# A step of the state-space scan: state increments ahead of the 64-column products, sums of squares behind them

## The chip, the core and the metric

The kernel runs on one core of a Trainium2 chip. The metric is the device time of one execution in microseconds. A core has five engines with queues of their own that run at the same time and wait for each other on semaphores: TensorE (PE, matrix products into PSUM), VectorE (DVE), ScalarE (ACT), GpSimd (POOL) and SyncE (SP, which here issues DMA transfers).

## The reference

One layer of a decoder trunk over 1024 tokens of width 1024. The part that the change touches is the chunked state-space scan (SSD), with 8 groups of 4 heads, head width 64, state 128:

```python
cb = jnp.einsum('bclgn,bcsgn->bcgls', cc, bc)
y_diag = jnp.einsum('bcgls,bcgrls,bcsgrp->bclgrp', cb, decay, xd)
decay_to_end = jnp.exp(a_cs[..., -1:] - a_cs)
chunk_states = jnp.einsum('bcsgn,bcgrs,bcsgrp->bcgrpn', bc, decay_to_end, xd)
...
    return state * cd[..., None, None] + cs, state          # scan over chunks
...
y_off = jnp.einsum('bclgn,bcgrpn,bcgrl->bclgrp', cc, prev_states, jnp.exp(a_cs))
y = y_diag + y_off
...
y_b = rms_norm(yz.reshape(..., SSM_GROUPS, -1), ssm_norm_w)  # yz = (y + x*d_skip) * silu(z)
merged = sigmoid(g_a) * (y_a @ w_proj_a) + sigmoid(g_b) * (y_b @ w_proj_b)
return x + gate * (merged @ w_out)
```

Chunks are 128 tokens long; B, C, x and z come from the input projection, which runs before.

## The kernel before

The program has a long first part (norm, input projection, convolution, gates; up to about 915 us), then the SSD stage (about 915 to 1145 us), then the projection of y_b and the output product. The change reorders instructions in the SSD stage and renames PSUM banks in it and behind it.

**Steps.** The stage has 32 steps, one for each of 8 groups and 4 spans of 256 tokens (two chunks). Groups go in pairs: `order` lists (g, s) with the two groups of a pair in turn. In step n the loop calls, for its own and for later steps, the pieces of class `Group`:

- `decay_rows` of step n+3: ACT's exponentials `ea`, and POOL's mask (an affine_select) on the tile `dcy` of decays;
- `front` of step n: PE forms `yi`, the products inside the chunks (8 of 64 columns, xd against dcy), and `sp`, the increments of the state (2 of 256 columns, bn against xe); DVE writes `y` from yi and x (two instructions) and adds the first half of sp to the state `st`; POOL multiplies the state by the next chunk's decay (`decayed`);
- a few pieces of the first projection, y_a @ w_proj_a (`draw`: pairs of products `pma` of 512 columns, 4 or 5 a step), which need nothing of the scan;
- `prep_xe` of step n+1: DVE makes `xe` (x times the decay to the end of the chunk) from the transposed x in PSUM (`px`), and frees px's bank;
- `back` of step n: PE forms `yn` from the states, DVE multiplies it by ea (`ym`), POOL adds it to y; DVE adds the second half of sp, POOL decays the state and makes `yz`; every second time `post` plans what follows from yz;
- `prep_products` of step n+2: PE forms C times B and transposes B (both into `pc`) and x (into `px`); DVE multiplies dcy by pc and makes `xd`;
- `decay_exps` of step n+3 and `prep_b` of step n+2: ACT's exponentials on dcy, and its copy `bn` of the transposed B;
- `fetch` of step n+6: SP loads dcy and the operands `sl`.

**Order.** PE and SP run in the order in which the code emits, and in this stage so do DVE, ACT and POOL (`Engine` keeps the program's order). The order of the code is thus the order on each engine; what waits, holds up all that is behind it on its engine. Two high-and-low pairs of the projection's weights are split beside the steps: `wah` by ACT, `wal` by DVE (two instructions, in six of the steps), and SP loads them.

**Tasks.** `later(delay, f)` plans f for `delay` items ahead; a step has three items (front, back, prep_products). `post` plans the squares of yz (ACT, and their sum on POOL), `post2` (PE: `pq`, the sums over channels, 4 products of 32 columns), then `post2b` (DVE: a row of sums into cwt, tri or par), the row's store to `ss_d` and load as `ssq` (SP), POOL's power, and the store to `rs_d`. The groups 6 and 7 have shorter delays (`soon = 4`).

**Banks.** PSUM has eight banks, held in the list `free`, which begins as BANKS. `bank(name)` takes the first of the list, `release` puts a bank at its end. A product into a bank therefore waits for whoever used the bank last, and a change of the order of `bank` and `release` changes who that is. Behind the stage, `places_of` says which bank each product of the second projection takes.

The line L91 of the profile is the helper `mm` (a product), L94 is `tp` (a transpose), L100 is `move` (a DMA on SP), and L56 is the wrapper through which DVE, ACT and POOL instructions are recorded, so there tiles tell them apart, not lines. A product of 32-bit operands shows as two rows on PE.

Of the kernel before, what the change touches and what calls it, by code (L numbers as in the profile page):

```python
# [8 lines left out]
F32 = mybir.dt.float32  # L9
# [3 lines left out]
ALU = mybir.AluOpType  # L13
# [3 lines left out]
P = 128  # L17
# [3 lines left out]
NCH = S // P  # L21
# [14 lines left out]
def hybrid_kernel(  # L36
# [21 lines left out]
    V, A, G, PE = Engine(nc.vector), Engine(nc.scalar), Engine(nc.gpsimd), nc.tensor  # L58
    ctx.enter_context(nc.allow_non_contiguous_dma(reason="small parameter vectors"))

    x, out = x[0], out[0]
# [23 lines left out]
    def cst(shape, name, dt=F32):  # L85
        return const.tile(shape, dt, name=name, tag=name)
# [3 lines left out]
    def mm(acc, l, r, first=True, last=True):  # L90
        pin(PE.matmul(acc, l, r, start=first, stop=last))  # L91

    def tp(dst, src, idn):
        pin(PE.transpose(dst, src, idn))  # L94
# [4 lines left out]
    def move(dst, src):  # L99
        pin(nc.sync.dma_start(dst, src))  # L100
# [6 lines left out]
    ident = cst([P, P], "ident")  # L107
# [21 lines left out]
    dskt = cst([P, 16], "dskt")  # L129
# [13 lines left out]

    hpool = tc.tile_pool(name="hpool", bufs=1, reuse_waits="tile")
    hp = hpool.__enter__()
    BANKS = (1, 4, 6, 0, 3, 5, 2, 7)
    BN = ("b11", "t1", "t2", "b22", "t3", "b21", "t4")
    bop = {}
    for nm in BN:
# [338 lines left out]
    def bank(name):  # L488

        if not free and not at_bank:  # L490
            return psum.tile([P, 512], F32, name=name, tag="bk", bufs=6)
        at_bank[name] = free.pop(0)
        return psum.tile([P, 512], F32, name=name, tag=f"k{at_bank[name]}")

    def release(*names):

        free.extend(at_bank.pop(name) for name in names if name in at_bank)

    def numbered(pool, c):
        for b in range(8):  # L500
            pool.tile([P, 512], F32, name=f"{c}{b}_0", tag=f"{c}{b}")
# [4 lines left out]
    def later(delay, f, *a):  # L506
        tasks.append((slot[0] + delay, f, a))
# [557 lines left out]
    class Group:  # L1065
# [50 lines left out]
        def prep_products(self, s):  # L1116
            g, nm = self.g, f"{self.g}_{s}"
            sl, dcy, ea = self.pre[s]
            px, pc = bank(f"px{nm}"), bank(f"pc{nm}")
            for i in range(2):  # L1120
                tsl = slice(i * P, (i + 1) * P)
                mm(pc[:, i * P : (i + 1) * P], sl[:, 1, tsl], sl[:, 0, tsl])
                tp(pc[:, 256 + i * P : 256 + (i + 1) * P], sl[:, 1, tsl], ident)
                tp(px[:, i * 256 : i * 256 + P], sl[:, 2, tsl], ident)
                tp(px[:, i * 256 + P : i * 256 + 256], sl[:, 3, tsl], ident)
            d3 = dcy.rearrange("p h i l -> p h (i l)")
            V.tensor_tensor(d3, d3, pc[:, 0:256].unsqueeze(1).to_broadcast([P, HPG, 256]), op=ALU.mult)
            self.raw[s] = px, pc
            self.xs[s] = [self.weighted(s, "xd", dthq)]
# [30 lines left out]
        def front(self, s):  # L1160

            g, nm = self.g, f"{self.g}_{s}"
            sl, dcy, ea = self.pre[s]
            bn, (xd, xe) = self.bn[s], self.xs[s]
            yi = bank(f"yi{nm}")
            for i in range(2):
                for h in range(HPG):
                    j, hh = h // 2, h % 2
                    mm(yi[hh * HD : (hh + 1) * HD, j * 256 + i * P : j * 256 + (i + 1) * P],
                       xd[:, i * 256 + h * HD : i * 256 + (h + 1) * HD], dcy[:, h, i, :])  # L1170
            sp = bank(f"sp{nm}")
            last = s == NCH // 2 - 1
            for i in range(1 if last else 2):
                mm(sp[:, i * 256 : (i + 1) * 256], bn[:, i * P : (i + 1) * P], xe[:, i * 256 : (i + 1) * 256])
            self.y[s] = y1 = turn(y1_r, f"y1{nm}", F32).rearrange("p (j t) -> p j t", j=2)
            for j in range(2):
                V.scalar_tensor_tensor(y1[:, j], sl[:, 2 + j], dskt[:, 2 * g + j : 2 * g + j + 1],
                                       yi[:, j * 256 : (j + 1) * 256], op0=ALU.mult, op1=ALU.add)
            self.sts = [self.st]
            if self.st is None:  # L1180
                self.st = self.state(f"st{nm}_0")
                V.tensor_copy(self.st, sp[:, 0:256])
            else:
                self.st = self.nxt
                V.tensor_add(self.st, self.st, sp[:, 0:256])
            self.sts.append(self.st)
            self.nxt = None
            release(f"yi{nm}")
            if last:
                release(f"sp{nm}")  # L1190
            else:
                self.nxt = self.state(f"st{nm}_1"), sp
                self.decayed(self.nxt[0], s, 1)
# [30 lines left out]
        def post(self, q):  # L1224

            g = self.g
            yz = self.yz[q]

            def leave():
                for j in range(2):  # L1230
                    move(yb_d[2 * g + j][:, q * 512 : (q + 1) * 512], yz[:, j])

            if g < NG - 2 or q == 0:
                soon = 0 if g < NG - 2 else 4
                later(4, leave)
                later(9 - soon, self.squares, yz, [yz[:, j] for j in range(2)])
                later(17 - 2 * soon, self.post2, q, yz[:, 0])
            else:
                wait = 1 if g < NG - 1 else 3
                later(wait + 3, leave)  # L1240
                sq = [turn(r, f"sq{g}", F32) for r in ((y1_r, ym_r) if g < NG - 1 else (war_r[0], war_r[0]))]
                later(wait, self.squares, yz, sq, pin)
                later(9, self.post2, q, sq[0])
# [71 lines left out]
    def take(name, tag=None, dt=F32R):  # L1315
        return hp.tile([P, 512], dt, name=name, tag=tag or room.pop(0))

    def ring(n):

        return [room.pop(0) for _ in range(n)], [0]  # L1320

    def turn(r, name, dt=F32R):
        tags, at = r
        at[0] += 1
        return take(name, tags[(at[0] - 1) % len(tags)], dt)
# [170 lines left out]
    tha_r, ea_r, y1_r, ym_r = (ring(c) for c in (4, 3, 2, 2))  # L1496
# [11 lines left out]
    numbered(psum, "k")  # L1508
    free.extend(BANKS)
    for k in (6, 7):  # L1510
# [249 lines left out]
    ps3 = tc.tile_pool(name="ps3", bufs=1, space=PSUM, reuse_waits="tile")  # L1760
    psb = ps3.__enter__()
    numbered(psb, "q")
    places_of = {"x": (1, 3, 2, 0), "y": range(4, 8)}
    assert all(b > 3 for b in free[6:])
    wo, wor = {}, {}
    KO = (4, 5, 6, 7, 0, 1, 2, 3)
# [90 lines left out]
    def inv_root(sq):  # L1857

        y, t, v = sq[:, 2:3], sq[:, 3:4], sq[:, 1:2]
        V.tensor_scalar(t, sq[:, 0:1], 1.0 / D, EPS, op0=ALU.mult, op1=ALU.add)  # L1860
        V.tensor_scalar(y.bitcast(I32), t.bitcast(I32), -0.5, float(0x5F3759DF), op0=ALU.mult, op1=ALU.add)
        V.tensor_scalar_mul(v, t, -0.5)
        for _ in range(3):
            V.scalar_tensor_tensor(t, y, y, v, op0=ALU.mult, op1=ALU.mult)
            V.scalar_tensor_tensor(y, t, 1.5, y, op0=ALU.add, op1=ALU.mult)
        return y
# [24 lines left out]
    for n, t in enumerate(tiles):  # L1891
        tsl = slice(t * P, (t + 1) * P)
# [5 lines left out]
        last = n == NCH - 1  # L1898
# [15 lines left out]
        if last:  # L1914
            V.scalar_tensor_tensor(sq[:, 0:1], part[:, 0:1], part[:, 1:2], part[:, 2:3], op0=ALU.add, op1=ALU.add)
            y = inv_root(sq)
# [4 lines left out]
        else:  # L1921
            V.tensor_add(r, pw, xr)
            A.activation(xr, r, AF.Square, accum_out=sq[:, 0:1])  # L1923
            y = inv_root(sq)
# [35 lines left out]
```

## Time and profile before

| | |
|---|---|
| median of 3 runs | 1393.12 us (1393.1 to 1395.72) |
| profiled execution | 1396.63 us |
| its span | 1394.9 us, granted clock 0.999 |
| PE busy | 1370.1 us (98%) |
| DVE / ACT / POOL busy | 1032.8 / 771.2 / 211.5 us |
| HBM read and written | 195.63 and 83.30 MB |

Busy time is the time in which an engine runs an instruction; the span is from the first to the last. An engine with a busy share near 100% sets the time; the idle time of the others is spent waiting, mostly for it. The timeline's columns are start, duration, engine, line, operation, output and inputs, size and count, and in brackets the idle time ahead of it, with what ended it.

### The profile page before, as it was taken

What the parts mean: (1) busy time and instruction counts of PE and PEld (TensorE: products, weight loads), DVE (VectorE), ACT (ScalarE), POOL (GpSimd) and SP (SyncE); (2) the same over time, 40 slices, a digit from 0 to 9 for tenths busy, and PEclk for the clock granted to TensorE, in tenths of its full rate; (3) what the DMA queues carried; (4) which work ended last, traced back from release to release, by engine and by line L of the source; (5) the groups of instructions that cost most, each with busy time, mean ns of one, the idle gap of its engine ahead of it and who ended that gap; (6) DMA issues with size and microseconds to landing.
All of it is one profiled execution on the core that took longest, in us unless ns stands there. A gap on an engine that the chain in (4) does not pass through costs nothing.

```text
span 1394.9 us, 20349 instructions
## 1 busy us (share of the span) xinstructions
PE 1370.1 (98%) x7015; PEld 1131.3 (81%) x7015; DVE 1032.8 (74%) x1771; ACT 771.2 (55%) x1420; POOL 211.5 (15%) x198
## 2 busy tenths in 40 slices
PE   8999999999999999999999999999999999999997
PEld 6678888888888888888888788888888878888886
DVE  4666766776677789878988877577888768787743
ACT  6664456566556666555656555577777724233301
POOL 0000000000000000000000010018888860000000
PEclk9999999999999999999999999999999999999999
DMA  8565533333322567677667876598899859987332
GB/s 265 154 223 160 176 110 112 108 99 111 117 91 91 158 183 210 208 245 241 207 207 219 253 226 178 179 333 294 290 316 293 261 148 294 411 263 273 136 121 76
DMA packets 268907, 280.28 MB, mean 201 GB/s; under 512 B 18396, under 2 KB 215428, under 8 KB 268804
## 3 DMA queue, kind: packets, MB, share of 16 engines
q1 hardware_dynamic: 193796, 211.20, 48.3%
q10 hardware_dynamic: 75008, 67.78, 14.3%
q8 instruction: 55, 0.90, 0.3%
q14 instruction: 48, 0.39, 0.1%
HBM read 195.63 MB, written 83.30 MB: 200 GB/s over the span
## 4 chain that ended last, share of the span: by engine, by line
PE 86%; DMA 4%; DVE 3%; ACT 2%; issue 2%; POOL 1%; SPq 1%; POOLq 0%; DVEq 0%; ACTq 0%
PE xx L591 6%; PE xuz L591 6%; PE xcb L591 6%; PE po L91 6%; PE xz L591 6%; PE xg L591 5%; PE x L1680 5%; PE pma L91 4%; PE yp L1680 3%; PE yuz L591 3%; PE ycb L591 3%; PE yx L591 3%; PE vx L703 3%; PE yz L591 3%; PE yg L591 3%; PE vy L703 2%
## 5 line engine op out<-in xcount | busy, mean ns | idle before, releaser
L923 POOL TENSOR_TENSOR wog<-wog,gb 128x1024 f32<-128x1024 f32 x8 | 22.6, 2830 | 647.1 <-DMA wbr<-in_w_proj_b_dram 450.0
L56 ACT ACTIVATE dcy<-dcy,nacs 128x128 f32<-128x128 f32 x256 | 78.3, 388 | 16.9 <-POOL dcy L56 16.4
L56 POOL TENSOR_SCALAR_AFFINE_SELECT dcy<-dcy 128x1024 f32<-128x1024 f32 x32 | 36.4, 1138 | 102.1 <-DVE yh L56 61.3
L91 PE MATMUL pma<-yh,wah 128*128 128x512 f32 x128 | 42.9, 416 | 0.0
L91 PE MATMUL pma<-yh,wal 128*128 128x512 f32 x128 | 42.6, 414 | 0.0
L56 ACT ACTIVATE ea<-dcy 64x512 f32<-64x512 f32 x64 | 40.3, 629 | 4.0 <-DMA dcy<-acs_d 3.5
L56 POOL TENSOR_TENSOR yz<-y,sl 128x512 f32<-128x512 f32 x32 | 41.3, 1290 | 0.6
L56 DVE TENSOR_TENSOR dcy<-dcy,pc 128x1024 f32<-128x1024 f32 x32 | 39.0, 1218 | 2.7 <-PE pc L94 1.8
L1014 ACT ACTIVATE ac<-ac 128x1024 f32<-128x1024 f32 x32 | 34.0, 1061 | 12.6 <-DVE ac L1012 12.4
L56 DVE TENSOR_TENSOR ym<-yn,ea 128x512 f32<-128x512 f32 (+1 forms) x32 | 19.9, 621 | 27.8 <-PE yn L91 27.7
L91 PE MATMUL pma<-yl,wah 128*128 128x512 f32 x128 | 39.9, 393 | 0.0
L56 POOL TENSOR_TENSOR y<-y,ym 128x512 f32<-128x512 f32 (+1 forms) x32 | 36.6, 1143 | 15.3 <-DVE ym L56 15.0
L91 PE MATMUL yi<-dcy,xd 128*64 128x128 f32 x512 | 35.0, 279 | 2.8 <-DVE xe L56 2.5
L1923 ACT ACTIVATE xr<-r 128x1024 f32<-128x1024 f32 x7 | 7.4, 1061 | 53.0 <-issue 39.0
L1012 DVE SCALAR_TENSOR_TENSOR ac<-c2x,cwt,ac 128x1023 f32<-128x1023 f32 (+2 forms) x24 | 30.7, 1280 | 7.7 <-ACT ac L1010 7.6
L1913 POOL TENSOR_TENSOR r<-r,fnw 128x256 f32<-128x256 f32 (+1 forms) x3 | 2.7, 915 | 219.0 <-ACT xr L1912 219.0
L1012 DVE SCALAR_TENSOR_TENSOR ac<-c2cb,cwt,ac 128x1023 f32<-128x1023 f32 (+2 forms) x24 | 30.7, 1281 | 6.1 <-ACT ac L1010 6.0
L91 PEld LDWEIGHTS yi<-dcy,xd 128*64 128x64 f32 x512 | 27.3, 136 | 9.1 <-issue 3.8
L56 DVE SCALAR_TENSOR_TENSOR yn<-yn,par,rb 128x512 f32<-128x512 f32 x32 | 24.4, 762 | 13.6 <-DMA yn<-yb_d 12.3
L91 PE MATMUL sp<-xe,bn 128*128 128x256 f32 x112 | 32.7, 409 | 0.0
L1012 DVE SCALAR_TENSOR_TENSOR ac<-c1cb,cwt,ac 128x1023 f32<-128x1023 f32 (+2 forms) x24 | 30.7, 1280 | 0.8 <-issue 0.8
L1012 DVE SCALAR_TENSOR_TENSOR ac<-c1x,cwt,ac 128x1023 f32<-128x1023 f32 (+2 forms) x24 | 30.7, 1281 | 0.0
(2837 smaller groups left out, 4370.2 us busy)
## 6 DMA issues: line engine op xcount, KB each, us to landing
sl<-s_d SPq DMA_DIRECT2D x32, 768.0 KB
s_d<-ac ACTq DMA_DIRECT2D x32, 512.0 KB
dcy<-acs_d SPq DMA_DIRECT2D x32, 512.0 KB
aw<-in_ada_w_dram SPq DMA_DIRECT2D x16, 512.0 KB
vp<-in_w_in_dram SPq DMA_DIRECT2D x32, 256.0 KB
wbr<-in_w_proj_b_dram SPq DMA_DIRECT2D x64, 128.0 KB
wb_d<-wbb ACTq DMA_DIRECT2D x32, 256.0 KB
wb_d<-wbc ACTq DMA_DIRECT2D x32, 256.0 KB
```

The costliest lines, as they stand in the source:

```text
L56: return lambda *a, **k: tc.keep_in_program_order(f(*a, **k))
L91: pin(PE.matmul(acc, l, r, start=first, stop=last))
L591: pin(PE.matmul(ps, lw[:, k * P : (k + 1) * P], r[k], start=first and n + k == 0, stop=n == 2 and k == 3, skip_group_check=not first))
L703: pin(PE.matmul(ps[j], l[k][:, js], r, start=first and k + m == 0, stop=k == 3 and m == 2, skip_group_check=not first))
L923: G.tensor_mul(w, w, gb)
L1012: V.scalar_tensor_tensor(ac[:, s:], cc[:, : S - s], conv_wt[:, 3 - s, i : i + 1], ac[:, s:], op0=ALU.mult, op1=ALU.add)
L1014: A.activation(ac, ac, AF.Silu)
L1680: pin(PE.matmul(ps[j], a[:, v, js], r, start=first and n + k == 0, stop=n == 2 and k == KT - 1, skip_group_check=not first))
L1913: G.tensor_mul(r[:, cs], r[:, cs], fnw[:, cs])
L1923: A.activation(xr, r, AF.Square, accum_out=sq[:, 0:1])
```

## The change

In `front`, the products of sp, and the addition to the state and the decay that follow from them, are emitted ahead of those of yi and of y's two instructions. In `prep_products`, both products pc lead, then both transposes of B, then the four of x. In `post`, post2 is planned one item later for groups 0 to 5 (18 instead of 17; for q = 0 of the others it stays 9), so that pq stands behind front's products instead of ahead of them. Two lists of banks are permuted.

```diff
-    BANKS = (1, 4, 6, 0, 3, 5, 2, 7)
+    BANKS = (1, 4, 6, 0, 3, 2, 5, 7)
...
                 mm(pc[:, i * P : (i + 1) * P], sl[:, 1, tsl], sl[:, 0, tsl])
-                tp(pc[:, 256 + i * P : 256 + (i + 1) * P], sl[:, 1, tsl], ident)
+            for i in range(2):
+                tp(pc[:, 256 + i * P : 256 + (i + 1) * P], sl[:, 1, i * P : (i + 1) * P], ident)
+            for i in range(2):
+                tsl = slice(i * P, (i + 1) * P)
                 tp(px[:, i * 256 : i * 256 + P], sl[:, 2, tsl], ident)
                 tp(px[:, i * 256 + P : i * 256 + 256], sl[:, 3, tsl], ident)
...
             bn, (xd, xe) = self.bn[s], self.xs[s]
+            sp = bank(f"sp{nm}")
+            last = s == NCH // 2 - 1
+            for i in range(1 if last else 2):
+                mm(sp[:, i * 256 : (i + 1) * 256], bn[:, i * P : (i + 1) * P], xe[:, i * 256 : (i + 1) * 256])
             yi = bank(f"yi{nm}")
             for i in range(2):
                 for h in range(HPG):
                     ...
-            sp = bank(f"sp{nm}")
-            last = s == NCH // 2 - 1
-            for i in range(1 if last else 2):
-                mm(sp[:, i * 256 : (i + 1) * 256], bn[:, i * P : (i + 1) * P], xe[:, i * 256 : (i + 1) * 256])
-            self.y[s] = y1 = turn(y1_r, f"y1{nm}", F32).rearrange("p (j t) -> p j t", j=2)
-            for j in range(2):
-                V.scalar_tensor_tensor(y1[:, j], sl[:, 2 + j], dskt[:, 2 * g + j : 2 * g + j + 1],
-                                       yi[:, j * 256 : (j + 1) * 256], op0=ALU.mult, op1=ALU.add)
             self.sts = [self.st]
...
                 V.tensor_add(self.st, self.st, sp[:, 0:256])
             self.sts.append(self.st)
             self.nxt = None
+            self.y[s] = y1 = turn(y1_r, f"y1{nm}", F32).rearrange("p (j t) -> p j t", j=2)
+            for j in range(2):
+                V.scalar_tensor_tensor(y1[:, j], sl[:, 2 + j], dskt[:, 2 * g + j : 2 * g + j + 1],
+                                       yi[:, j * 256 : (j + 1) * 256], op0=ALU.mult, op1=ALU.add)
             release(f"yi{nm}")
...
-                later(17 - 2 * soon, self.post2, q, yz[:, 0])
+                later(18 - 9 * soon // 4, self.post2, q, yz[:, 0])
...
-    places_of = {"x": (1, 3, 2, 0), "y": range(4, 8)}
+    places_of = {"x": (3, 1, 2, 0), "y": range(4, 8)}
```

PE in the step whose yi starts at 1057.11 us in the trace; in a name the digits before the last number are group and step (`yi4_2`: group 4, step 2), the last number counts tiles. Before:

```order
L91 MATMUL pc5_2_10207<-sl5_2_9989 128x128
L94 MATMUL pc5_2_10207<-ident_144,sl5_2_9989 128x128
L94 MATMUL px5_2_10206<-ident_144,sl5_2_9989 128x128 x2
L91 MATMUL pc5_2_10207<-sl5_2_9989 128x128
L94 MATMUL pc5_2_10207<-ident_144,sl5_2_9989 128x128
L94 MATMUL px5_2_10206<-ident_144,sl5_2_9989 128x128 x2
L91 MATMUL pq2_1_10219<-yz2_2_9620,ones_149 32x128 x4
L91 MATMUL yi4_2_10244<-dcy4_2_9894,xd4_2_10137 64x128 x8
L91 MATMUL sp4_2_10253<-xe4_2_10190,bn4_2_10147 128x256 x2
L91 MATMUL pma4_0_9934<-yh50_8372,wal4_1_9605 128x512
```

And now:

```order
L91 MATMUL pc5_2_10207<-sl5_2_9983 128x128 x2
L94 MATMUL pc5_2_10207<-ident_144,sl5_2_9983 128x128 x2
L94 MATMUL px5_2_10206<-ident_144,sl5_2_9983 128x128 x4
L91 MATMUL sp4_2_10239<-xe4_2_10188,bn4_2_10147 128x256 x2
L91 MATMUL yi4_2_10242<-dcy4_2_9889,xd4_2_10137 64x128 x8
L91 MATMUL pq2_1_10257<-yz2_2_9617,ones_149 32x128 x4
L91 MATMUL pma4_0_9931<-yh50_8372,wal4_1_9602 128x512
```

The narrow products (yi 64 columns wide, pq 32) now stand together, behind sp and ahead of pma.

DVE in the same step, from the making of xe on. Before:

```order
L56 TENSOR_TENSOR xd5_2_10217<-px5_2_10206,dthq_160 128x512
L56 SCALAR_TENSOR_TENSOR y14_2_10256<-sl4_2_9896,dskt_158,yi4_2_10244 128x256 x2
L56 TENSOR_TENSOR st_home_8488<-st_home_8488,sp4_2_10253 128x256
L56 TENSOR_SCALAR tri_151<-pq2_1_10219 128x128
L56 TENSOR_TENSOR xe5_2_10277<-px5_2_10206,dde_161 128x512
L56 TENSOR_TENSOR ym4_2_10285<-yn4_2_10279,ea4_2_9898 128x512
L56 TENSOR_TENSOR st4_2_1_10260<-st4_2_1_10260,sp4_2_10253 128x256
L56 TENSOR_TENSOR dcy4_3_10073<-dcy4_3_10073,pc4_3_10295 128x1024
```

And now:

```order
L56 TENSOR_TENSOR xd5_2_10217<-px5_2_10206,dthq_160 128x512
L56 TENSOR_TENSOR st_home_8488<-st_home_8488,sp4_2_10239 128x256
L56 SCALAR_TENSOR_TENSOR y14_2_10252<-sl4_2_9891,dskt_158,yi4_2_10242 128x256 x2
L56 TENSOR_TENSOR xe5_2_10274<-px5_2_10206,dde_161 128x512
L56 TENSOR_TENSOR ym4_2_10282<-yn4_2_10276,ea4_2_9893 128x512
L56 TENSOR_TENSOR st4_2_1_10255<-st4_2_1_10255,sp4_2_10239 128x256
L56 TENSOR_SCALAR tri_151<-pq2_1_10257 128x128
L56 TENSOR_TENSOR dcy4_3_10072<-dcy4_3_10072,pc4_3_10295 128x1024
```

The state's addition changed places with y, and the row of sums went from ahead of xe to behind the second addition.

At the end of the stage, PE ahead of the last pc (`pc7_3`). There the bank of pc7_3 was pq5_1's, which DVE reads into cwt; now it is that of px6_3, which DVE reads into xe6_3. The rows themselves only show the order; now:

```order
L91 MATMUL pc7_3_11047<-sl7_3_10816 128x128 x2
L94 MATMUL pc7_3_11047<-ident_144,sl7_3_10816 128x128 x2
L94 MATMUL px7_3_11046<-ident_144,sl7_3_10816 128x128 x4
L91 MATMUL sp6_3_11061<-xe6_3_11029,bn6_3_10986 128x256
L91 MATMUL yi6_3_11063<-dcy6_3_10736,xd6_3_10973 64x128 x8
L91 MATMUL pq7_0_11076<-yz7_0_10703,ones_149 32x128 x4
```

On SP, the stores of the rows of sums go behind the next fetches of dcy and sl; on POOL the power of ssq goes from ahead of y's addition to behind yz, ahead of the next mask. No engine's count of instructions changes.

## The prediction

> **What bounds the kernel now.** First the head of the page, then the busy time by windows of the span: 915 to 1145 us is the SSD stage, the only one whose instructions the change moves. The window's row gives its length and then, each with its count, the busy time of PE, PEld, DVE, ACT and POOL.
>
> ```profile
> span 1394.9 us, 20349 instructions
> PE 1370.1 (98%) x7015; PEld 1131.3 (81%) x7015; DVE 1032.8 (74%) x1771; ACT 771.2 (55%) x1420; POOL 211.5 (15%) x198
> 915.00:1145.00 230.00, 224.11 (x1702) 187.56 (x1701) 181.24 (x311) 157.22 (x397) 175.44 (x171) 1.00 0.85 281
> ```
>
> TensorE (PE) is busy 98% of the span, and in the stage 224.11 of 230.00 us, at the full granted clock (1.00). So two things can change the time: how long PE's own stream is, and the 230.00 - 224.11 = 5.89 us in which PE stands still. The waits of the stage, third (total us, times, longest), say who waits:
>
> ```profile
> DVE ym L56 <- PE yn L91: 27.7, 23, 4.3
> POOL dcy L56 <- ACT ea L56: 39.8, 14, 21.4
> PE yi L91 <- DVE xe L56: 2.5, 2, 1.5
> DVE dcy L56 <- PE pc L94: 1.8, 6, 0.4
> PE yn L91 <- POOL st_home L56: 1.5, 2, 1.0
> PE px L94 <- ACT bn L56: 0.9, 1, 0.9
> ```
>
> DVE stands behind PE in 23 of 32 steps, 27.7 us; PE behind another engine only a handful of times. The bound is PE's stream, with few places at which DVE sets the pace for a moment.
>
> **PE's own stream.** PE's timeline of a step without sums of squares, in groups (start, duration); what counts is the distance from start to start, since a matmul's tail lies under the next.
>
> ```profile
> 992.91 0.38 PE L94 MATMUL px<-ident,sl 128*128 128x128 f32 x2
> 993.13 0.39 PE L91 MATMUL pc<-sl 128*128 128x128 f32 x2
> ...
> 993.47 0.38 PE L94 MATMUL px<-ident,sl 128*128 128x128 f32 x2
> 993.78 1.09 PE L91 MATMUL yi<-dcy,xd 128*64 128x128 f32 x16
> 994.80 1.13 PE L91 MATMUL sp<-xe,bn 128*128 128x256 f32 x4
> 995.58 0.81 PE L91 MATMUL pma<-yh,wal 128*128 128x512 f32 x2
> 996.23 0.63 PE L91 MATMUL pma<-yh,wah 128*128 128x512 f32 x2
> ```
>
> Two px transposes take 0.22 to the next full-width group (992.91 to 993.13) but 0.31 to the 64-column yi (993.47 to 993.78). Then yi 1.02, sp 0.78, the first pma pair 0.65. From px to the second pma pair: 0.31 + 1.02 + 0.78 + 0.65 = 2.76 us.
>
> The new order is px, sp, yi, pma. It runs nowhere before, so its pieces come from two places late in the stage where the 32-column pq follows sp, and one where pq stands ahead of yi:
>
> ```profile
> 1113.01 0.43 PE L91 MATMUL pq<-yz,ones 128*32 128x128 f32 x8
> 1113.36 1.09 PE L91 MATMUL yi<-dcy,xd 128*64 128x128 f32 x16
> 1114.38 1.13 PE L91 MATMUL sp<-xe,bn 128*128 128x256 f32 x4
> 1115.45 0.42 PE L91 MATMUL pq<-yz,ones 128*32 128x128 f32 x8
> 1115.81 0.72 PE L91 MATMUL pma<-yh,wah 128*128 128x512 f32 x2
> 1116.37 0.63 PE L91 MATMUL pma<-yl,wah 128*128 128x512 f32 x2
> ...
> 1122.91 0.70 PE L91 MATMUL sp<-xe,bn 128*128 128x256 f32 x2
> 1123.54 0.43 PE L91 MATMUL pq<-yz,ones 128*32 128x128 f32 x8
> ```
>
> Four sp between narrow neighbours take 1.07 and two take 0.63, so one costs (1.07 - 0.63)/2 = 0.22 and the two changes of width on either side 0.63 - 0.44 = 0.19, about 0.10 each. Entering from full width saves one: 0.97. A pma pair behind a narrow group takes 0.56. So the new step is 0.22 + 0.97 + 1.02 + 0.56 = 2.77 us: 0.01 more a step, within the rounding of the rows. I take 32 x 0.01 = +0.3 us, bounded by 0.02 of rounding either way: -0.3 to +0.9. If entering sp from full width saved nothing, it would be 2.87, +3.5 us in all; that is a rival below.
>
> In steps with pq, the block costs 0.35 ahead of yi (1113.01 to 1113.36) and, ahead of pma, 0.36 (1115.45 to 1115.81): moving it from before yi to behind yi costs nothing. Only in the step at 1113 do two pq blocks, which stood on both sides of yi and sp, become neighbours: one block of 16 rows, without the two changes of width around one of them and with both ends of the other, saves about 0.4. That saving stays under DVE's wait at the stage's end (below), so I count it at 0; it is worth -0.4 if that cover goes.
>
> [...] The sum goes by the rows.
>
> The new order of pc and px only exchanges full-width groups of equal pitch: 0 on PE. It does let DVE's dcy start after PE's sixth instead of its eighth instruction of the ten, 0.22 earlier, where it waits (1.8 us in 6 visible waits). DVE then waits for yn instead (27.7 us): worth something only where xe is late.
>
> **Where sp now needs xe sooner.** Before, sp began 1.02 behind yi; now it begins where yi did. DVE makes xe early unless it first has a pair of wal to do, which happens at six places. At four of them xe ends before PE wants it or nearly so, as here (DVE's timeline, then PE's):
>
> ```profile
> 981.66 1.22 DVE L56 TENSOR_TENSOR dcy<-dcy,pc 128x1024 f32<-128x1024 f32 x1 [0.36 <-PE pc L94]
> ...
> 984.51 0.28 DVE L56 TENSOR_SCALAR tri<-pq 128x128 f32<-128x128 f32 x1
> 984.71 2.47 DVE L56 TENSOR_TENSOR wal<-wa,wah 128x512 fp32r<-128x512 f32 x2
> 987.10 0.68 DVE L56 TENSOR_TENSOR xe<-px,dde 128x512 f32<-128x512 f32 x1
> ...
> 987.11 0.38 PE L94 MATMUL px<-ident,sl 128*128 128x128 f32 x2
> ```
>
> xe ends at 987.78, sp would be due at 987.11 + 0.22 = 987.33: 0.45 late. But DVE no longer does the row of sums ahead of wal (tri: 984.51 to 984.71, 0.20), and dcy starts 0.22 earlier: 0.42 back. I take 0, at most +0.45. The same holds for the step at 1084. The fifth place is one where PE waits already, with pq filling part of the time (PE's timeline; then a row of SP's and one of POOL's, used below):
>
> ```profile
> 1055.68 0.43 PE L91 MATMUL pq<-yz,ones 128*32 128x128 f32 x8
> 1057.11 1.09 PE L91 MATMUL yi<-dcy,xd 128*64 128x128 f32 x16 [1.00 <-DVE xe L56]
> ...
> 1043.80 0.49 SPq L100 DMA_DIRECT2D ss_d<-cwt  x1
> ...
> 1056.89 1.01 POOL L56 TENSOR_TENSOR ssq<-ssq,nhalf 128x4 f32<-128x4 f32 x1
> ```
>
> Here yi's bank was freed by xe, so yi and now sp start at the same 1057.11. But pq, done before the wait, now comes behind yi: 0.36 more, and sp pays 0.10 for yi's change of width: about +0.45. Against it stands that DVE is late here because of a chain from SP's fetch of dcy, and the store of an earlier row of sums now goes behind that fetch on SP's queue; I credit 0.35 of its 0.49 us of issue and take +0.1, bounds -0.4 to +0.45.
>
> **The stage's end** is the sixth place. PE's and DVE's timelines:
>
> ```profile
> 1114.98 0.42 DVE L56 TENSOR_TENSOR st<-st,sp 128x256 f32<-128x256 f32 x1 [3.44 <-POOL st L56]
> ...
> 1118.36 2.87 DVE L56 TENSOR_TENSOR wal<-wa,wah 128x512 fp32r<-128x512 f32 x2
> 1121.15 0.68 DVE L56 TENSOR_TENSOR xe<-px,dde 128x512 f32<-128x512 f32 x1
> ...
> 1119.12 0.39 PE L91 MATMUL pc<-sl 128*128 128x128 f32 x2
> 1120.00 0.38 PE L94 MATMUL px<-ident,sl 128*128 128x128 f32 x2
> 1121.88 1.09 PE L91 MATMUL yi<-dcy,xd 128*64 128x128 f32 x16 [1.50 <-DVE xe L56]
> ...
> 1131.74 0.68 PE L91 MATMUL yn<-sl,st_home 128*128 128x128 f32 x4 [0.44 <-DVE st_home L56]
> ```
>
> DVE hangs on POOL until 1114.98, so xe ends at 1121.83, or 0.20 earlier, since the row of sums ahead of this wal goes too: 1121.63. Before, PE did the last B and C products (1119.12 on) under this wait. Now those products take the bank that xe frees, and wait too. They cost 0.88 + 0.22 = 1.10, then two sp 0.22 + 0.31, yi 1.02, pq 0.36, pma 0.56: the second pma pair comes at about 1125.2 against 1121.88 + 1.02 + 0.63 + 0.36 + 0.56 = 1124.45: +0.75. The wait of yn at 1131.74 (0.44) then has nothing to wait for, and a small later one of pq on POOL goes with it: +0.2, bounds -0.2 to +0.75. The wait of px for bn (0.9) shrinks, since three more pc instructions stand ahead of px, but DVE's 1114.98 comes next: 0. The two waits for POOL's st_home stay: POOL does a mask right ahead of it, and that is not moved.
>
> POOL's power of ssq (1.01 at 1056.89, in 14 steps) moves from ahead of y's addition to ahead of the next mask. POOL waits there for ACT's ea, 39.8 us in 14 places: hidden, at worst 1.0 at one place without cover. The state's addition ahead of y's two instructions brings POOL's state forward and y back by 0.33; with yi ending 0.97 later y comes later, under DVE's wait for yn: 0.
>
> **The sum.** +0.3 (order on PE) +0 (merged pq) +0.1 (1057) +0 (984, 1084) +0.2 (end) = +0.6 us. The profiled execution took 1396.63 us (span 1394.9 and 1.7 around it), 3.5 over the median of the runs shown, and would become 1397.2; on the median, 1393.12 + 0.6 = 1393.7. Own range, from the bounds: -1.3 to +3.0. A measurement of this kernel can tell about 0.2%, 2.8 us, from no change.
>
> **The rivals.**
> Waits go: the state is formed about 0.9 earlier, xe follows wal without the row of sums, and so the few waits of PE vanish. At most 5.89 us, 1387.2; half of it, 1390, to be told from no change. For it: both large waits hang on DVE's xe. Against: at these two nothing in the new order makes xe over 0.2 to 0.4 earlier, and sp needs it sooner. 0.2.
> sp waits for xe at every wal: 1.00 as at 1057 at the four places without a wait now, with 0.45 at 1057 and 0.75 at the end, +5.2, 1398.3. It decides from 0.4 a place on top of these two (2.8 us in all). wal took 2.47 and 2.87 in the two rows, so 0.4 comes from nothing more than what stands beside it. Against: xe's margin, 0.2 us and DVE's earlier dcy. 0.15. [...]
> Changes of width cost more in the new order: sp between full width and yi 1.07 instead of 0.97, 32 x 0.11 = +3.5, 1396.6. For it: no row shows this order. Against: both widths were met singly. 0.1.
> The forecast, that PE's stream is as long as before and the waits trade places, has 0.55.
>
> Range for 8 in 10: from half of the waits gone to the changes of width, 1390.0 to 1397.2. Faster by over 0.2% is the first rival, 0.2; slower the second and third, 0.25; within it 0.55.
>
> **What would show it.** Right: PE's busy time in the stage within 1 us of 224.11; px to sp 0.22, sp to yi 0.97, yi to pma 1.02, the first pma pair 0.56; the wait for xe now under sp, at 1057 and at the end under pc. Wrong: over 0.5 us of PE idle ahead of sp at the other wal places (second rival), a step of over 2.85 (third), or a stage with under 3 us of PE idle (first).

## The result, and the profile after

| | before | changed |
|---|---|---|
| median of the first comparison (12 runs each) | 1396.57 us | 1404.23 us, ratio 1.0056 (95% interval 1.0036 to 1.0075) |
| median of a second one | 1392.9 us | 1402.54 us, ratio 1.0067 (1.0054 to 1.0080) |
| span of the profiled executions | 1394.9 us | 1409.3 us; in the second comparison 1398.4 us |

The changed kernel is 8 to 10 us slower, where +0.6 was forecast and 1397.2 was the upper end of the range. Its first profiled execution was the slowest of its twelve runs and 3.5 us late already where the stage begins, which the change doesn't touch; so the second one is read beside it.

The order on PE came out as laid out beforehand. PE's timeline of a plain step of the changed kernel:

```profile
997.21 0.60 PE L94 MATMUL px<-ident,sl 128*128 128x128 f32 x4
997.64 1.03 PE L91 MATMUL sp<-xe,bn 128*128 128x256 f32 x4
998.60 1.09 PE L91 MATMUL yi<-dcy,xd 128*64 128x128 f32 x16
999.63 0.74 PE L91 MATMUL pma<-yh,wal 128*128 128x512 f32 x2
1000.20 0.62 PE L91 MATMUL pma<-yh,wah 128*128 128x512 f32 x2
```

From px (two of its four) to the second pma pair it is 0.22 + 0.96 + 1.03 + 0.57 = 2.78 us, where 2.77 was worked out. PE's busy time in the stage (window, then PE, PEld, DVE, ACT, POOL) is the same too, 224.27 against 224.11:

```profile
918.50:1151.00 232.50, 224.27 (x1701) 184.46 (x1700) 179.98 (x311) 156.77 (x397) 173.10 (x171) 1.00 0.84 278
```

What is new are waits, one of them behind the stage, where the prediction did not look. The waits of the changed kernel, 915 to 1160 us:

```profile
PE x L1683 <- DVE tri L56: 5.5, 1, 5.5
PE px L94 <- ACT bn L56: 2.0, 1, 2.0
PE pc L91 <- issue: 1.9, 1, 1.9
PE sp L91 <- DVE xe L56: 1.8, 2, 1.2
PE yn L91 <- POOL st_home L56: 1.3, 2, 0.7
PE pq L91 <- DVE st L56: 0.8, 1, 0.8
```

The largest is that of x, the second projection's products right behind the stage. PE's timelines there, before and then changed; the row with the wait is the first product into the fourth tile, x3:

```profile
1146.87 0.39 PE L1680 MATMUL x<-p1bh,p1a 128*128 128x512 f32 x1
1147.50 0.50 PE L1680 MATMUL x<-p1bh,p1a 128*128 128x512 f32 x1 [0.24 <-DVE cwt L56]
1147.83 0.40 PE L1680 MATMUL x<-p1bl,p1a 128*128 128x512 f32 x1
1148.07 0.63 PE L1680 MATMUL x<-p1bh,p1a 128*128 128x512 f32 x2
```

```profile
1153.09 0.39 PE L1683 MATMUL x<-p1bh,p1a 128*128 128x512 f32 x1
1158.94 0.79 PE L1683 MATMUL x<-p1bh,p1a 128*128 128x512 f32 x1 [5.46 <-DVE tri L56]
1159.53 0.63 PE L1683 MATMUL x<-p1bl,p1a 128*128 128x512 f32 x1
1159.95 1.06 PE L1683 MATMUL x<-p1bh,p1a 128*128 128x512 f32 x2
```

x3 takes bank 0 in both kernels. Before, bank 0 held the last but one row of sums (pq6_1, read by DVE into cwt); with the new order of requests and the new BANKS it holds the very last (pq7_1, read into tri). DVE's timeline shows what lies between the two, changed kernel:

```profile
1153.04 0.28 DVE L56 TENSOR_SCALAR cwt<-pq 128x128 f32<-128x128 f32 x1
1156.72 0.75 DVE L56 SCALAR_TENSOR_TENSOR yn<-yn,par,rb 128x512 f32<-128x512 f32 x1 [3.40 <-DMA yn<-yb_d]
1157.39 0.69 DVE L56 TENSOR_TENSOR p1bl<-yn,p1bh 128x512 fp32r<-128x512 f32 x1
1158.00 0.68 DVE L56 TENSOR_TENSOR p1a<-p1r,p1a 128x512 fp32r<-128x512 f32 x1
1158.60 0.28 DVE L56 TENSOR_SCALAR tri<-pq 128x128 f32<-128x128 f32 x1
```

Between cwt and tri DVE waits for a load and prepares an operand. PE's 512-column products waited for a bank that DVE was to read behind all that. And the products behind the wait are slow: 0.42 from start to start (1159.53 to 1159.95), 0.24 before. The windows of the same place give the reason (length, PE busy, granted clock, DMA share):

```profile
1153.50:1158.90 5.40, 0.00 (x0) 0.88 0.95 333
1158.90:1161.90 3.00, 2.96 (x7) 0.50 0.62 209
1161.90:1164.50 2.60, 2.60 (x7) 0.50 0.71 113
1164.50:1168.00 3.50, 3.50 (x16) 1.00 1.01 358
```

After 5.4 us of idle time the granted clock is 0.50 for 5.6 us. If half of that time is lost, which is an estimate from the clock and from the 0.42 against 0.24, it costs 2.8 us on top of the wait. In other profiles the clock was 0.50 after idle times of 4.00 (e6) and 4.80 us (the changed kernel a second time) as well, and after the 1.88 ahead of pc here it was 1.00; but after 1.9 us ahead of pc in e1, e3 and e8 below it was 0.50 too (last section).

### The profile page after: what moved, and what is told of

It reads as the page before. It is cut to its first block, busy times and chain, and to the rows that moved or that the text cites. A ratio compares the mean times of both kernels' runs of the same rounds, so it can differ in the third digit from the quotient of the medians.

```text
span 1409.3 us, 20364 instructions
## 1 busy us (share of the span) xinstructions
PE 1374.2 (98%) x7015; PEld 1129.8 (80%) x7015; DVE 1030.2 (73%) x1771; ACT 771.2 (55%) x1420; POOL 208.9 (15%) x198
## 4 chain that ended last, share of the span: by engine, by line
PE 77%; DMA 10%; DVE 3%; ACT 3%; POOL 2%; issue 2%; SPq 2%; POOLq 0%; ACTq 0%; DVEq 0%
PE xuz L591 6%; PE xx L591 6%; PE xcb L591 6%; PE xz L591 5%; PE yp L1683 5%; PE po L91 5%; PE xg L591 4%; PE x L1683 4%; PE yuz L591 3%; PE vx L703 3%; PE pma L91 3%; PE yx L591 3%; DMA dcy<-acs_d 3%; PE ycb L591 3%; PE yz L591 3%; PE yg L591 2%
## 5 line engine op out<-in xcount | busy, mean ns | idle before, releaser
L91 PE MATMUL sp<-xe,bn 128*128 128x256 f32 x112 | 29.7, 382 | 1.9 <-DVE xe L56 1.8
```

## The experiments

The theories: **A**, the loss is mostly the bank of x3 (its wait and the slow clock behind it), the rest a few microseconds in the stage; **B**, the order inside the stage costs it. Each kernel ran with the kernel before on the same chip. The table has the parts of each profiled execution, worked out from the starts of PE's rows: the stage (last product of the input projection to last pma), the second projection (first x to first po) and po (first to last).

| kernel | ratio to before (95% interval) | stage | second projection | po |
|---|---|---|---|---|
| before | 1 | 224.20 | 154.19 | 87.53 |
| changed, first and second | 1.0056, 1.0067 | 226.91, 225.62 | 161.00, 159.02 | 88.93, 87.51 |
| e1 | 1.0107 (1.0094 to 1.0120) | 228.04 | 152.57 | 101.72 |
| e2 | 1.0172 (1.0159 to 1.0185) | 224.03 | 176.44 | 89.76 |
| e3 | 1.0057 (1.0042 to 1.0072) | 227.94 | 158.70 | 87.49 |
| e4 | 1.0137 (1.0124 to 1.0150) | 227.39 | 168.45 | 89.85 |
| e5 | 1.0022 (1.0010 to 1.0033) | 225.88 | 152.58 | 90.05 |
| e6 | 1.0054 (1.0040 to 1.0068) | 223.73 | 159.53 | 87.92 |
| e8 | 1.0058 (1.0046 to 1.0070) | 227.96 | 158.05 | 87.53 |
| e9 | 1.0012 (1.0001 to 1.0023) | 224.84 | 152.61 | 88.36 |
| e10 | 1.0014 (1.0002 to 1.0026) | 226.36 | 152.57 | 87.48 |
| e11 | 1.0000 (0.9989 to 1.0010) | 223.10 | 152.58 | 87.50 |
| e12 | 1.0011 (1.0000 to 1.0022) | 225.35 | 152.59 | 88.37 |

In five of these profiles the clock fell inside the stage as well: in e1, e3 and e8 behind the wait ahead of the last pc (1.9 us), in e4 and e5 behind the wait of px (2.8 and 1.9), each time to 0.50 for 3.4 us. In the other nine it stayed at 1.00 through the stage. In e1, e3 and e8 the way from that pc to the next pma took 4.70 us instead of 3.08, so 1.6 us of their stage is this clock. In e4 and e5 later waits are shorter by as much: from the px that waits to the first pma behind the last pc it is 12.46 us in e5, and 12.48 and 12.46 in the two profiles of the changed kernel; from that px to the sp behind the last px it is 9.80 in e4, and 9.80 in e9.

**e1, e2: other places for x, a first attempt.** e1 is the changed kernel with the places in order of release, e2 the kernel before with x3 on the last row's bank.

```diff
e1:
-    places_of = {"x": (3, 1, 2, 0), "y": range(4, 8)}
+    places_of = {"x": tuple(free[:4]), "y": tuple(free[4:])}
e2:
-    places_of = {"x": (1, 3, 2, 0), "y": range(4, 8)}
+    places_of = {"x": (1, 3, 2, 4), "y": (0, 5, 6, 7)}
```

> The changed kernel with one edit: behind the SSD stage the second projection takes the PSUM banks in the order in which they came free, so that its fourth tile x3 no longer gets the bank of the last row of sums. Theory A (the bank, then the clock): in the changed kernel x3 waits 5.46 us for DVE's row of sums tri, and PE then runs at a granted clock of 0.50 for about 5.4 us, which costs 2.6 more; without the wait both go, so 7.8 us below the changed kernel, a ratio to before of 0.998 to 1.002. Rival B (the order inside the SSD stage costs the time): the wait at x3 is paid for elsewhere, the ratio stays at 1.004 to 1.007.

> The kernel before with one edit: the second projection's x3 takes the bank of the last row of sums (y takes the one that x3 had); the SSD stage is untouched. Theory A: x3 waits until DVE's row tri at about 1152 instead of cwt at 1147, 4.8 us more, and with the half clock behind it 2.4 more: 7 us slower than before, ratio 1.004 to 1.006. Rival B: within 1 us of before.

Both missed by far, because the edit did more than it should. In e1 the wait of x3 was gone, but a larger one stood further down; the first line below is of e1, the others of e2:

```profile
PE po L91 <- DVE tg L56: 12.5, 1, 12.5
```

```profile
PE po L91 <- DVE tg L56: 15.1, 1, 15.1
PE x L1680 <- DVE tri L56: 5.3, 1, 5.3
```

The output product po takes banks 4 to 7, which y has emptied by then; with x on one of them po waits for x's last reader. A bank has a successor as well as a predecessor. The times of e1 and e2 therefore tell nothing on A; the parts do: without the late bank the second projection of e1 took 152.57 us, and e2's stage took 224.03, as before, with a wait of 5.3 at x3.

**e3, e8: the idle time filled.** 24 products without use ahead of x3, into a bank of y that is overwritten later (e8 is e3 again, beside the changed kernel):

```diff
+            if u == 0 and j == 3:
+                for _ in range(24):
+                    pin(PE.matmul(psy[2], a[:, 0, 0:P], bh, start=True, stop=True))
```

> The changed kernel with 24 products of no use (into a bank that is overwritten later) ahead of x3, so that PE is busy through the time in which it waited for tri: 24 x 0.23 = 5.5 us. Theory A with the clock falling because PE stood still: the granted clock stays at 1.00, x3 starts when it did, and 2.6 us come back: ratio to before about 1.0037 instead of 1.0056. If the fall of the clock has nothing to do with the idle time: no gain, ratio 1.0056.

> The kernel with 24 useless products ahead of x3 once more, now beside the changed kernel on the same chip. If PE's idle time lowers the granted clock: 2 to 2.6 us below the changed kernel, clock 1.00 behind x3. If not: the same time.

The clock stayed up: e3's windows over the filled time, and behind it, and the row at which x3 starts:

```profile
1148.50:1153.90 5.40, 5.40 (x24) 1.00 0.96 303
1153.90:1156.00 2.10, 1.73 (x9) 1.00 0.97 356
```

```profile
1154.27 0.50 PE L1686 MATMUL x<-p1bh,p1a 128*128 128x512 f32 x1 [0.37 <-DVE tri L56]
```

But the time did not move: 1402.35 us (e8) against 1402.54 for the changed kernel beside it. In the profiles the second projection is shorter, 158.70 and 158.05 us against 161.00 and 159.02, but part of the gain went elsewhere. In e3 tri itself came later, so that x3 started 8.0 us behind the first x (1146.26 to 1154.27), against 7.0 in the second profile of the changed kernel (1143.70 to 1150.70). In e8 the products ran 0.4 us past the end of tri. And the stage was 2.3 us longer in both than in that profile, 1.6 of it by the slow clock at its end. So the windows show that here it was the idle time that lowered the clock (0.50 behind it, 1.00 with the time filled); that avoiding it pays was not shown.

**e4: front's order alone**, with e1's places, and so with the wait of po (15.7 us):

> The kernel before with only the order inside front changed (sp and the state ahead of yi and y), and the banks behind the stage in the order in which they came free; order of pc and px, and the sums' delay, as before. Theory A: the order inside the stage is worth within 2 us of before, ratio 0.9985 to 1.0015. Rival B: most of the change's loss, ratio 1.003 to 1.006.

Its time tells nothing for the reason given at e1; its stage was 227.39 us. The same order stands in e9 with other banks.

**e5, e6: banks renamed.** Here only names are exchanged, so that x has banks of 0 to 3 and y of 4 to 7, and the one that differs is the bank of the last row of sums: it is y's in e5 (the changed kernel) and x3's in e6 (the kernel before).

```diff
e5:
-    BANKS = (1, 4, 6, 0, 3, 2, 5, 7)
+    BANKS = (1, 4, 0, 6, 3, 2, 5, 7)
-    places_of = {"x": (3, 1, 2, 0), "y": range(4, 8)}
+    places_of = {"x": (2, 1, 0, 3), "y": range(4, 8)}
e6:
-    BANKS = (1, 4, 6, 0, 3, 5, 2, 7)
+    BANKS = (1, 0, 6, 4, 3, 5, 2, 7)
```

> The changed kernel with two banks renamed (0 and 6 exchanged in BANKS, x at 2, 1, 0, 3), so that x takes the four banks that come free first, all of 0 to 3, and the last row of sums ends on a bank of y; nothing else moves. Theory A (two causes: the bank of x3, and some 3.8 us in the SSD stage): the wait of x3 and the half clock go, the SSD stage stays 3.8 us longer, so +2 to +4 us against before, ratio 1.0015 to 1.003, 4 to 6 us below the changed kernel of the same call. Rival B (all of it is the stage): ratio stays at the changed kernel's. Rival C (all of it is the bank): ratio 0.998 to 1.001.

> The kernel before with two banks renamed (0 and 4 exchanged in BANKS), so that x3 takes the bank of the last row of sums and the product behind keeps its banks; the SSD stage is untouched. Theory A: a wait of about 5 us at x3 and a granted clock of 0.50 behind it, 5 to 8 us slower than before, ratio 1.0035 to 1.0055. Rival B: ratio 1.000.

> The changed kernel once more, beside the others on the same chip: ratio 1.0056 as measured, between 1.0036 and 1.0075. Theory A expects the wait of x3 in its profile again, at 3 to 6 us, and the half clock behind it.

(e7 is the changed kernel again, the second one of the table.) Theory A holds on both sides: e5 is at 1.0022 where the changed kernel beside it is at 1.0067, so the bank costs some 0.45% or 6.3 us (in the profiles 6.4, 159.02 against 152.58 for the second projection); and e6, whose stage is untouched, is at 1.0054. What is left of e5's loss, 0.22% or 3.1 us, is not the stage alone: against before, its profile has +1.7 in the stage, -1.6 in the second projection and +2.5 in po, with a wait of 1.0 for DVE among it that nothing here explains. PE's rows and windows of e6 around x3:

```profile
1144.12 0.39 PE L1680 MATMUL x<-p1bh,p1a 128*128 128x512 f32 x1
1148.51 0.80 PE L1680 MATMUL x<-p1bh,p1a 128*128 128x512 f32 x1 [4.00 <-DVE tri L56]
```

```profile
1144.50:1148.50 4.00, 0.01 (x1) 0.87 0.98 342
1148.51:1154.25 5.74, 5.74 (x14) 0.50 0.74 219
```

Two numbers in BANKS, with no instruction added or moved, make the kernel before 0.5% slower: a 4.00 us wait and 5.7 us at a clock of 0.50, 6.9 in all if half of the 5.7 is lost (the estimate from above). Its second projection, at 159.53 us, is 7.0 longer than the 152.57 or 152.58 of e1, e10 and e11, where x3 does not wait.

**e9 to e12: the parts of the stage.** e9 has front's order alone, e10 the later sums alone, e11 the order of pc and px alone, each with the banks named so that, as in e5, x takes the four that come free first. e12 is e5 with pc taking its bank ahead of px in the last step:

```diff
+            if nm == "7_3":
+                pc, px = bank(f"pc{nm}"), bank(f"px{nm}")
+            else:
                 px, pc = bank(f"px{nm}"), bank(f"pc{nm}")
```

> The kernel before with only the order inside front changed, the banks named so that x takes the four that come free first, all of 0 to 3. Theory A1 (within the stage, front's order costs most of the 1.5 to 3.8 us that the stage grew by, since sp now stands right behind xe): stage (last product of the input projection to the last pma) 226.5 to 227.5 us against 224.2, ratio 1.000 to 1.0025. Rival A2 (the later sums of squares cost it, through SP's stores and the bank of pc): stage 224.0 to 225.0, ratio 0.998 to 1.000.

> The kernel before with only the sums of squares planned one item later, banks as in e9. Theory A1: stage within 1 us of 224.2, ratio 0.998 to 1.001. Rival A2: stage 226 to 228, ratio 1.001 to 1.003; in its profile pc at the end of the stage waits for the bank of xe.

> The kernel before with only B's and C's products ahead of the transposes of x, banks as in e9. Both theories: DVE's dcy starts 0.22 earlier and the wait of px for bn shrinks, nothing else: stage 223.5 to 224.3, ratio 0.998 to 1.000. It would be the version to keep if the ratio is under 0.999.

> e5 (the changed kernel with the banks renamed) with one edit more: in the last step pc takes its bank ahead of px, so that the products for pc no longer wait for xe, only the transposes for px. Theory A: the wait ahead of pc at the end of the stage (1.3 to 1.9 us) gives 0.66 us back, six products of 0.11: stage 0.66 shorter than with e5's order, ratio 1.001 to 1.002. If that wait had another cause: the same wait of 1.3 to 1.9 ahead of pc.

e9 and e10 both come out 0.1% slower, with intervals that only just leave out 1. The stages fit A2 in both (e9 224.84, e10 226.36) and A1 in neither; but A2 had e9 no slower than before, so neither is the whole. Front's order added 0.6 us to the stage in this profile, the later sums 2.2. In e4, with the same order, it was 3.2; there px waited 2.8 us for bn, here 0.4. Each alone also adds changes of width, 0.10 each by the prediction's estimate, that the two together don't have (in e9 pq, sp, yi stand in turn, in e10 yi, sp, pq). e10 shows where the later sums cost at the end, and e12 that this is pc's bank (lines of e10, then of e12):

```profile
PE pc L91 <- issue: 1.9, 1, 1.9
```

```profile
PE px L94 <- ACT bn L56: 1.6, 1, 1.6
PE px L94 <- DVE xe L56: 1.2, 1, 1.2
```

The wait ahead of pc turned into one of 1.2 ahead of px, for xe, whose bank px now has. The stage of e12 was 0.5 us shorter than e5's; 0.66 was expected. Single profiles of the same stage differ by up to 2.4 us (225.62 to 228.04), but the stretch around this wait doesn't: from the px that waits for bn to the first pma behind the last pc it is 11.96 us in e12, and 12.46 to 12.48 in e5 and the two profiles of the changed kernel. e11 is level with before, and its stage in one profile was 1.1 us shorter. No version was measurably faster than the kernel before.

## Why the prediction was wrong, step by step

**The step that failed is the first:** the SSD stage as "the only one whose instructions the change moves", from which the sum has no term for anything behind it. No instruction behind it moves, but the two permuted lists say who held a bank last, and the products behind the stage wait for that. The prediction followed banks inside the stage to the last pc and stopped there. In the kernel before the same wait is in sight (x3 behind cwt, 0.24 us), and DVE's rows there show tri 4.75 us behind cwt:

```profile
1147.16 0.28 DVE L56 TENSOR_SCALAR cwt<-pq 128x128 f32<-128x128 f32 x1
1150.04 0.75 DVE L56 SCALAR_TENSOR_TENSOR yn<-yn,par,rb 128x512 f32<-128x512 f32 x1 [2.60 <-DMA yn<-yb_d]
1151.91 0.28 DVE L56 TENSOR_SCALAR tri<-pq 128x128 f32<-128x128 f32 x1
```

That one step would have given +4.75, and the slow clock some 2 to 3 more, an estimate from the 5.6 us at 0.50 in the changed kernel's profile. Against before, the second projection of the two profiles is longer by 4.8 and 6.8 us (159.02 and 161.00 against 154.19, which has short waits of its own); against e5, where only the bank differs, the term is 6.4 and 8.4, and the ratios of e5 and the changed kernel put it at 6.3. Most of the loss is thus outside the sum.

**PE's own stream:** right, 2.78 against 2.77 a step, so the third rival (changes of width dearer) is out.

**sp and xe:** the place was right, the size a little low. The wait at 1057 went from yi to sp, and two more appeared:

```profile
945.46 1.10 PE L91 MATMUL sp<-xe,bn 128*128 128x256 f32 x4 [0.67 <-DVE xe L56]
...
1061.18 1.10 PE L91 MATMUL sp<-xe,bn 128*128 128x256 f32 x4 [1.16 <-DVE xe L56]
```

At 984 us of before (991 here) sp started 0.28 late (the two rows below, px's 4 x 0.108 = 0.43), where 0 was taken and 0.45 was the bound. The wait at 945 was not in the sum, but the wait of yn next to it in the kernel before is shorter in return. The wait at 945 stands in a step without wal (xe there follows dcy and xd at once), so the prediction's search, which went by wal, could not find it. The second rival wanted 1.00 at each of the four wal places without a wait before; they had 0.28 in all, and 1057 had 1.16 (0.83 in the second profile) instead of 1.00. It is out; that the kernel did get slower has another cause.

```profile
990.55 0.60 PE L94 MATMUL px<-ident,sl 128*128 128x128 f32 x4
991.26 0.91 PE L91 MATMUL sp<-xe,bn 128*128 128x256 f32 x3
```

**The wait of px for bn:** taken to shrink (0.9, with three more products ahead of it); it grew instead, 1.98 us in this profile, 1.4 to 1.9 in the other profiles of the changed stage. Its chain goes back over ACT, which waits for the store of yz to leave, to SP. SP's rows, before and then changed:

```profile
1103.16 0.38 SPq L100 DMA_DIRECT2D ssq<-ss_d  x1
1103.59 1.49 SPq L100 DMA_DIRECT2D yb_d<-yz  x2
```

```profile
1107.95 1.38 SPq L100 DMA_DIRECT2D ssq<-ss_d  x1
1109.39 0.90 SPq L100 DMA_DIRECT2D yb_d<-yz  x2
```

Counted from the stage's beginning (920.63 and 924.14), the store is issued at 182.96 before and at 185.25 now, and at 184.32 in the second profile. Of these 2.29 and 1.36 us, 1.00 and 0.84 are the issue of the load ahead of it (1.38 and 1.22 us instead of 0.38); the rest is there already when SP gets past POOL's yz to the fetch of sl. The prediction had only credited a fetch that goes earlier; who stood behind the load was not asked. Why the wait grew stays open: the issue of this load also took 1.50 us in e11, which leaves the sums where they were, and 1.47 in e10, which moves them, and yet px waited only 0.2 and 0.7 there (0.4 in e9). And e4, with e9's stage, had a wait of 2.8, and e2, with the old stage, 2.1.

**The stage's end:** right in kind: pc waits for xe's bank (1.88), and yn's wait of 0.44 is gone. The short wait of pq for POOL is still there (0.3), and the double block of pq, counted at 0, now waits 0.82 for DVE's st, which was not in the sum. The net of +0.2 is lost in the spread of single profiles. In all, the six profiles of the changed stage average 227.1 us and the three of the old one (before, e2, e6) 224.0: +3.1, of which the slow clock in e1, e3 and e8 makes 0.8. The changed kernel's own two profiles average 226.3: +2.3, where the sum had +0.6 with an upper bound of +3.0. The stage alone would thus have stayed within the bounds.

## What to carry to other kernels

A buffer's name ties it to the one that used it last and to the one that uses it next, across the border of a stage: for every renamed or reordered buffer follow both to the end, in the order of releases, and ask where the last reader stands in its engine's queue. A short wait of the bottleneck engine that is just met (0.24 us here) is a warning: look what follows the releaser on its queue, since that is the price when the tie slips by one. And when an engine's order is moved, list who stands behind each moved transfer, not only what goes earlier.

## What was not expected of the hardware

TensorE's granted clock fell behind idle time within the kernel: waits of 4.00 (e6), 4.80 and 5.46 us (the changed kernel, second and first profile) brought a clock of 0.50 for about 5.7, 2.9 and 5.6 us behind them. Against the 152.58 us of e5 the second projection was 7.0, 6.4 and 8.4 us longer, 1.3 to 1.7 times the length of the wait.

The length of a wait did not decide alone. The waits ahead of the last pc are equal, 1.91 us, in e3 and in the second profile of the changed kernel, but only in e3 did the clock fall. The fall inside the stage lasted 3.41 us, and if each profile is cut into pieces of that length from one of its changes of clock, the two waits lie differently: in e3 the whole wait is in one piece, in the other it is split between two. Windows of e3, then of the second changed profile (length, PE busy, granted clock, DMA share):

```profile
1118.35:1121.76 3.41, 1.50 (x14) 1.00 0.02 1
1121.76:1125.17 3.41, 3.41 (x23) 0.50 0.13 37
```

```profile
1116.02:1119.43 3.41, 2.12 (x14) 1.00 0.02 1
1119.43:1122.84 3.41, 2.79 (x32) 1.00 0.02 6
```

The piece ahead of the fall has PE busy 1.50 or 1.51 us in e1, e3, e5 and e8 and 1.10 in e4, and the piece of e1 that begins at 1298.66, with 1.57, left the clock at 1.00. So in these pieces the clock fell where PE had stood still for 1.90 us or more, and held where it was 1.84. That the clock goes by such pieces is the author's estimate from these profiles; no run moved a wait across a border to try it.

Busy time alone hides the slow clock here: the slow products count as busy (2.96 of 3.00 and 2.60 of 2.60 us at 0.50, in the windows of the result), and PE's busy time of the first changed profile is 4 us higher than before (1374.2 against 1370.1) with the same 7015 instructions.

```profile
span 1409.3 us, 20364 instructions
PE 1374.2 (98%) x7015; PEld 1129.8 (80%) x7015; DVE 1030.2 (73%) x1771; ACT 771.2 (55%) x1420; POOL 208.9 (15%) x198
```
